# A decoder layer on one core: the first block's logits on 128 keys, and the MLP norm's factor applied after the second product

## The chip, the core and the metric

The kernel runs on one core of one Trainium2 chip. The metric is the device time of one execution in microseconds. The core has a matrix engine (TensorE, PE in the profile; PEld is its loading of weights), a vector engine (VectorE, DVE), a scalar engine for activations (ScalarE, ACT), GpSimd (POOL) and a queue that mostly issues DMAs (SyncE, SP). They run side by side and wait for each other through semaphores.

## What is computed

The layer takes 512 tokens of 1024 channels in float32. Two branches read the same RMS-normalised input: a chunkwise mLSTM with four heads, and sliding-window attention with 16 query heads, 4 key heads and learned sinks. They are merged through sigmoid gates and a projection, then come a squared-ReLU MLP, a gated per-layer embedding, and a final norm. The parts that the change touches are:

```python
def rmsnorm(x, g):
    xf = x.astype(jnp.float32)
    xf = xf * lax.rsqrt(jnp.mean(xf * xf, axis=-1, keepdims=True) + EPS)
    return xf.astype(x.dtype) * g.astype(x.dtype)

# attention: W = 128, nb = S // W = 4 blocks of queries, each against the block before and its own
logits = jnp.einsum("bnqhgd,bnkhd->bnhgqk", qb, kb).astype(jnp.float32) * (SW_HEAD_DIM ** -0.5)
diff = qi + W - ki
band_mask = (diff >= 0) & (diff < W)
valid = band_mask[None] & ((jnp.arange(nb)[:, None, None] > 0) | (ki >= W)[None])
...
# MLP
u = rmsnorm(x, norm_mlp_g[i]) @ w_up[i]              # 1024 -> 4096
x = x + jnp.square(jax.nn.relu(u)) @ w_down[i]       # 4096 -> 1024
```

The first block of queries (n = 0) has no block before it, so only the 128 keys of its own block count. In the MLP the norm's factor of a token, r = 1/sqrt(mean(x^2) + eps), is positive and the same for all channels of that token. So relu(r u)^2 = r^2 relu(u)^2, and r^2 may also multiply a token's sums after the second product.

## The kernel before

**Precision.** Nearly every large product is made from two float32r parts of each operand, a high part and the remainder. `split` makes them: ACT copies the high part (L134), DVE subtracts (L135). `pairs` lists three products per pair of tiles (high by high, high by low, low by high), and `chain` (L162) issues them all, so that one line stands for most matmuls. `load_w` loads a tile of weights and splits it; raw tiles have four buffers, and so have the parts `wh` and `wl`.

**Order.** The source's order is not the order on the engines. The tile framework plans each engine's stream from the dependencies, the free buffers and its own estimates of durations. `tc.keep_in_program_order` pins an instruction behind all that its engine has got so far, and `tc.issue_after` queues a group behind a given instruction.

**Attention.** There are 16 units: two pairs of key heads (`kp`), four blocks of 128 queries (`n`), two halves (`ab`). `swa_probs` makes the logits of one unit into a PSUM tile `ls` of 1024 columns, 256 for each of four query heads: one matmul with the high part of the keys (L608) and one with the low part (L609) per head, both over 256 keys whatever `n` is. The width `W` of what is read afterwards is 128 for n = 0 and 256 otherwise: the masked maximum on DVE (L616), the exponentials on ACT (L627), the division. `swa_out` transposes the probabilities (L645) and multiplies them by the values (L653). The units are started two ahead, with projections of other parts as filling between them.

**MLP.** Before it, `columns_of` transposes the residual `xk` (four views of the tile `XK`, 128 tokens each) and makes `x1`, scaled by the norm's gain but not by the token's factor. L852 to L860 then compute that factor: squares with a sum on ACT (L856), square root and reciprocal (`rstd_of`), a diagonal matrix from it on DVE (L858), and four products of `ones` with the diagonals (L859) that spread the factors along the columns of a PSUM tile. A copy (L860) puts them into `rB`, 128x512.

The MLP runs in four stages q, each with a first product (`up`, 1024 of the 4096 hidden channels in eight chunks of 128) and a second product (`down`). One chunk of `up` is 24 matmuls into one of two PSUM banks `psg`. L879 evicts the bank on DVE, with the relu and the factor in one instruction:

```python
V.scalar_tensor_tensor(a, ps, 0.0, rB, ALU.max, ALU.mult)
```

ACT squares the result into `F` (L883), and after every second chunk DVE makes four sums and differences in `F`, and `split` makes the operand `uf` from it. `F` has one buffer.

`down` computes a 2x2 block product with seven block products (Strassen's scheme in Winograd's form), on PSUM pairs X, Y and Z of 2 x 512 columns. When a pair holds something that belongs to a result block, `acc` adds it to the residual in one addition of 1024 columns (L916). One partial product, `p1`, is summed over all four stages in SBUF and added three times in the last stage (`acc_p1`); those additions are pinned. After the first product of the last stage, `ple_rows` loads the rows of the input `p` into memory that the MLP's scratch (`F` and `rt`) has left, and transposes them.

`cp` is the pool of small tiles that live throughout. Behind its constants it holds an unused tile `pad`.

Of the kernel before, what the change touches and what calls it, by code (L numbers as in the profile page):

```python
# [10 lines left out]
F32 = mybir.dt.float32  # L11
F32R = mybir.dt.float32r
AF = mybir.ActivationFunctionType
ALU = mybir.AluOpType
AX = mybir.AxisListType

P = 128
S = 512
D = 1024
NT = S // P  # L20
KT = D // P
EPS = 1e-6
# [14 lines left out]
def block_kernel(  # L37
# [30 lines left out]
    V, A, G, T = nc.vector, nc.scalar, nc.gpsimd, nc.tensor  # L68


    def pool(stack, name, **kw):
        return stack.enter_context(tc.tile_pool(name=name, bufs=1, reuse_waits="tile", **kw))
# [3 lines left out]
    cp = pool(ctx, "cp")  # L76
# [9 lines left out]
    def nm(s):  # L86
        n_names[0] += 1
        return f"{s}_{n_names[0]}"
# [8 lines left out]
    def ps_a():  # L97
        return pp.tile([P, 1024], F32, tag="a", bufs=2, name=nm("psa"))
# [26 lines left out]
    def small(n, w, bufs=4):  # L125
        return cp.tile([P, w], F32, tag=f"{n}{w}", bufs=bufs, name=nm(n))
# [27 lines left out]
    def pairs(a, b):  # L154

        return [(a[0], b[0]), (a[0], b[1]), (a[1], b[0])]
# [36 lines left out]
    ident = cp.tile([P, P], F32, name="ident")  # L193
    make_identity(nc, ident)
    ones = cp.tile([P, P], F32, name="ones")
    V.memset(ones, 1.0)
    eps_t = cp.tile([P, 1], F32, name="eps_t")

    cp.tile([P, 24], F32, name="pad")
    V.memset(eps_t, EPS)  # L200
    zeros4 = c1.tile([4, P], F32, name="zeros4")
    V.memset(zeros4, 0.0)
# [49 lines left out]
    def rstd_of(ss, n):  # L252

        w = ss.shape[1]
        sd = small("sd", w)
        A.activation(sd, ss, AF.Sqrt, bias=eps_t, scale=1.0 / n)
        rs = small("rs", w, 5)
        V.reciprocal(rs, sd)
        return rs
# [5 lines left out]
    for m in range(NT):  # L265
        xn = tok_scratch("xn")
        ss = small("ss", 1)
        A.activation(xn, xt[m], AF.Square, accum_out=ss)
        rs = rstd_of(ss, D)
        for c in range(2):  # L270
            o = slice(c * 512, (c + 1) * 512)
# [4 lines left out]
        for kq in range(2):  # L276
            ps = ps_t()
# [8 lines left out]
        ps = ps_g()  # L286
        for c in range(3):
            mm_tok(ps[:, :264], wv[c], hT[K3[c]], m, first=c == 0, last=c == 2)
        t = sp.tile([P, 256], F32, tag="vs", bufs=4, name=nm("vs"))
# [12 lines left out]
    kk, kl = [], []  # L302
    for i in range(2):
        ps = proj_T(w_ksw, i, ps_t)
        both = [act_r("kk"), act_r("kk")]
        low = [act_r("kl"), act_r("kl")]
        for ab in range(2):
            s, o = HALF[ab], HALF[1 - ab]
# [67 lines left out]
    for m in range(NT):  # L376
        t = tk("vm").rearrange("p (h d) -> p h d", h=NH)
# [223 lines left out]

    def swa_probs(kp, n, ab):
        k0 = max(n - 1, 0) * P
        ls = ps_a()
        for g in range(4):
            q = qs[kp * 4 + g, ab]
            o = ls[:, g * 256 : (g + 1) * 256]
            T.matmul(o, q[:, n * P : (n + 1) * P], kk[kp][ab][:, k0 : k0 + 256], start=True, stop=False)  # L608
            T.matmul(o, q[:, n * P : (n + 1) * P], kl[kp][ab][:, k0 : k0 + 256], start=False, stop=True)  # L609
        W = P if n == 0 else 2 * P  # L610
        kv = 2 * kp + ab
        sk = sink[:, kv * 4 : kv * 4 + 4]
        lm3 = tok_scratch().rearrange("p (g k) -> p g k", g=4)[:, :, :W]
        mx = small("mx", 4)
        for g in range(4):
            V.tensor_tensor_reduce(  # L616
                lm3[:, g, :], ls[:, g * 256 : g * 256 + W], band[:, 256 - W :], 0.125, sk[:, g : g + 1], ALU.add, ALU.max, mx[:, g : g + 1]
            )
        nmx = small("nmx", 4)
        V.tensor_scalar_mul(nmx, mx, -1.0)  # L620
        ds = small("ds", 4)
        V.tensor_sub(ds, sk, mx)
        es = small("es", 4)
        A.activation(es, ds, AF.Exp)
        sm = small("sm", 4)
        for g in range(4):
            A.activation(lm3[:, g, :], lm3[:, g, :], AF.Exp, bias=nmx[:, g : g + 1], accum_out=sm[:, g : g + 1])  # L627
        V.tensor_add(sm, sm, es)
        rc = small("rc", 4)
        V.reciprocal(rc, sm)  # L630
        V.tensor_tensor(lm3, lm3, rc.unsqueeze(2).broadcast_to([P, 4, W]), ALU.mult)
        probs[kp, n, ab] = lm3
# [153 lines left out]
    for i in range(8):  # L786
        ps = ps_g()
# [13 lines left out]
    XK = xp.tile([P, NT, D], F32, name="xk")  # L801
    xk = [XK[:, m, :] for m in range(NT)]
# [3 lines left out]
    def pair():  # L806

        return pp.tile([P, 2, 512], F32, tag="pair", bufs=3, name=nm("psp"))
# [13 lines left out]
    for nh in range(2):  # L822
        if nh == 0:
            a, b = pair(), pair()
            pv = [a[:, 0, :], a[:, 1, :], b[:, 0, :], b[:, 1, :]]
        else:
            a = pair()
# [5 lines left out]
        for m in range(NT):  # L833
            o = xk[m][:, nh * 512 : (nh + 1) * 512]
# [10 lines left out]
    mp = pool(st_m, "mp")  # L845
    F = lambda: mp.tile([P, 8, 256], F32, tag="F", bufs=1, name=nm("F"))

    A21, A11, A22, A12, S1, S2, S3, S4 = range(8)
    rB = mp.tile([P, 512], F32, name="rB")
    p1 = np_.tile([P, 2, 512], F32, name="p1")  # L850

    psr = pair()[:, 0, :]  # L852
    for m in range(NT):
        junk = np_.tile([P, 7 * 256], F32, tag="uf", bufs=8, name=nm("junk"))[:, :D]
        ss = small("ss", 1)
        A.activation(junk, xk[m], AF.Square, accum_out=ss)  # L856
        dg = mp.tile([P, 512], F32, tag="rt", bufs=3, name=nm("dg"))[:, :P]
        V.tensor_scalar_mul(dg, ident, rstd_of(ss, D))  # L858
        T.matmul(psr[:, m * P : (m + 1) * P], ones, dg, start=True, stop=True)  # L859
    A.copy(rB, psr)  # L860

    def load_down(q):
        raws = []
# [9 lines left out]
    def up(q, uf):  # L873
        fs = None
        for f in range(8):
            ps = ps_g()
            mm_T(ps, load_w(w_up[q * 8 + f], KT * P, KT), x1)
            a = mp.tile([P, 512], F32, tag="rt", bufs=3, name=nm("rt"))
            V.scalar_tensor_tensor(a, ps, 0.0, rB, ALU.max, ALU.mult)  # L879
            if f % 2 == 0:  # L880
                fs = F()
            o = 2 * (f % 2)
            A.activation(fs[:, o : o + 2, :].rearrange("p a b -> p (a b)"), a, AF.Square)  # L883
            if f % 2:
                hl = [np_.tile([P, 7 * 256], F32R, tag="uf", bufs=8, name=nm("uf")) for _ in range(2)]

                cut = 3 * 256 if f == 7 else 0
                if cut:
                    split([t[:, :cut] for t in hl], fs[:, 1:4, :].rearrange("p a b -> p (a b)"))
                V.tensor_add(fs[:, S1, :], fs[:, A21, :], fs[:, A22, :])  # L890
                V.tensor_sub(fs[:, S3, :], fs[:, A11, :], fs[:, A21, :])
                V.tensor_sub(fs[:, S2, :], fs[:, S1, :], fs[:, A11, :])
                V.tensor_sub(fs[:, S4, :], fs[:, A12, :], fs[:, S2, :])  # L893
                split([t[:, cut:] for t in hl], fs[:, 1 + cut // 256 :, :].rearrange("p a b -> p (a b)"))
                uf.append(hl)

    def down(q, uf):
        raws = load_down(q)
        b11, b12, b21, b22 = [[raws[4 * kh + i] for kh in range(2)] for i in range(4)]
        X, Y, Z = pair(), pair(), pair()  # L900

        def form(raw):
            return load_w(None, 1024, 2, raw)

        def prod(ps, a, w, kh, first, last):

            for t in range(2):
                o = (a - 1) * 256 + t * P
                ops = []
                for k in range(2):  # L910
                    ops += pairs([h[:, o : o + P] for h in uf[2 * kh + k]], [h[:, k, :] for h in w])
                chain(ps[:, t, :], ops, first and kh == 0, last and kh == 1, True)

        def acc(ps, toks, n):
            o = XK[:, 2 * toks : 2 * toks + 2, n * 512 : (n + 1) * 512]
            return V.tensor_add(o, ps, o)  # L916

        def acc_p1(toks, n):
            if q == 3:
                tc.keep_in_program_order(acc(p1, toks, n))  # L920

        for kh in range(2):
            V.tensor_sub(b12[kh], b22[kh], b12[kh])
        for kh in range(2):
            w = form(b11[kh])
            prod(X, A11, w, kh, True, False)
            V.tensor_add(b11[kh], b12[kh], b11[kh])
            w = form(b11[kh])
            prod(Y, S2, w, kh, True, False)
        if q == 0:  # L930
            A.copy(p1, X)
        else:
            V.tensor_add(p1, X, p1)
        acc(Y, 1, 1)
        for kh in range(2):
            w = form(b21[kh])
            prod(X, A12, w, kh, False, True)
            V.tensor_sub(b21[kh], b21[kh], b11[kh])
        acc(X, 1, 0)
        for kh in range(2):  # L940
            prod(Y, S3, form(b12[kh]), kh, False, False)
        acc(Y, 0, 1)
        acc_p1(0, 1)
        for kh in range(2):
            V.tensor_sub(b11[kh], b22[kh], b11[kh])
            prod(Z, S1, form(b11[kh]), kh, True, False)
        acc(Z, 0, 1)
        acc_p1(1, 1)
        acc_p1(0, 0)
        for kh in range(2):  # L950
            prod(Y, A22, form(b21[kh]), kh, False, True)
        acc(Y, 0, 0)
        for kh in range(2):
            prod(Z, S4, form(b22[kh]), kh, False, True)
        acc(Z, 1, 1)
# [51 lines left out]
    with tc.issue_after(evicted):  # L1007
        for m in range(NT):
            junk = tp.tile([P, D], F32, tag="junk", bufs=1, name=nm("junk"))
            ss = small("ss", 1)  # L1010
# [54 lines left out]
    a, b = pair(), pair()  # L1065
# [14 lines left out]
    for m in range(NT):  # L1080
        for o in (0, 256):
            ps = ps_g()[:, :256]
# [102 lines left out]
```

## Time and profile before

| | |
|---|---|
| median of three runs | 908.59 us (907.73, 908.59, 1108.4) |
| the profiled execution | 907.79 us, span 906.0 us |
| mean granted TensorE clock in it | 0.997 |
| TensorE busy | 890.4 us, 98% of the span |
| DVE, ACT busy | 640.6 us (71%), 452.8 us (50%) |
| traffic with HBM | 91.30 MB read, 8.40 MB written |

All durations below come from the one profiled execution, so they are to be set against its 907.79 us. Its span of 906.0 us is what the trace covers; the remaining 1.8 us lie around it. A share of busy time is an average over stages: what one stage is limited by is read in that stage. In the timelines a row has its start and its duration in microseconds, the engine, the line of the kernel, the operation, the tile written and the tiles read, and in brackets how long the engine was idle before it and what ended that.

### The profile page before, as it was taken

The numbers are of one execution on the slowest core, as the hardware profiler recorded it, in microseconds if no ns is written. First come the engines' busy times: TensorE is split into PE (matmuls) and PEld (weight loads), VectorE is DVE, ScalarE is ACT, GpSimd is POOL, SyncE is SP. The second block draws the span as 40 slices with busy tenths as digits, with TensorE's granted clock in tenths as the row PEclk, the third lists the DMA queues.
The fourth block names the chain that finished last, engine by engine and source line by source line (L and its number), as shares of the span: only waits on it lengthen the run. The fifth ranks groups of instructions, "written<-read, shape, count | busy, mean of one in ns | idle before, by whom it ended". The sixth has DMA issues, their size and how long they took to land.

```text
span 906.0 us, 11754 instructions
## 1 busy us (share of the span) xinstructions
PE 890.4 (98%) x4490; PEld 739.4 (82%) x4490; DVE 640.6 (71%) x1020; ACT 452.8 (50%) x757; POOL 25.0 (3%) x44
## 2 busy tenths in 40 slices
PE   7999999999999999999999999999999999999996
PEld 5888889998877677777888888888888888888886
DVE  6684687874787977466654678857966895799556
ACT  6573444454677567564322545334434533454753
POOL 0011000000000000000210000000000000000000
PEclk9999999999999999999999999999999999999998
DMA  6644124435211122234452520531162044201402
GB/s 235 241 156 151 59 81 167 162 117 173 71 49 69 47 96 92 76 110 140 163 186 93 207 95 1 198 127 47 54 225 94 0 159 146 69 24 64 145 1 93
DMA packets 30346, 101.51 MB, mean 112 GB/s; under 512 B 4301, under 2 KB 4813, under 8 KB 30290
## 3 DMA queue, kind: packets, MB, share of 16 engines
q1 hardware_dynamic: 28002, 93.15, 29.9%
q0 software_dynamic: 2144, 7.35, 2.3%
q8 instruction: 35, 0.57, 0.2%
q10 hardware_dynamic: 144, 0.26, 0.1%
q14 instruction: 21, 0.17, 0.1%
HBM read 91.30 MB, written 8.40 MB: 110 GB/s over the span
## 4 chain that ended last, share of the span: by engine, by line
PE 93%; ACT 2%; DVE 2%; DMA 1%; issue 0%; SPq 0%; ACTq 0%; DVEq 0%
PE psg L162 51%; PE psp L162 23%; PE psa L162 10%; PE pst L724 2%; PE pst L653 1%; PE pst L162 1%; PE psa L645 1%; PE pst L714 1%; PE psa L608 1%; PE psa L609 1%; DMA xt<-in_x 1%; DMA gfin<-in_g_fin 1%; PE psp L817 1%; ACT jk L736 1%; ACT pT L647 0%
## 5 line engine op out<-in xcount | busy, mean ns | idle before, releaser
L134 ACT CAST wh<-wr 128x1024 fp32r<-128x1024 f32 (+1 forms) x137 | 142.9, 1046 | 207.7 <-PE psg L162 75.4
L135 DVE TENSOR_TENSOR wl<-wr,wh 128x1024 fp32r<-128x1024 f32 (+1 forms) x137 | 173.4, 1270 | 102.4 <-ACT wh L134 95.4
L162 PE MATMUL psg<-x,wh 128*128 128x512 f32 x512 | 158.4, 390 | 0.0
L162 PE MATMUL psp<-wh,uf 128*128 128x512 f32 x448 | 139.2, 390 | 0.0
L162 PEld LDWEIGHTS psg<-x,wh 128*128 128x128 f32 x512 | 96.1, 188 | 19.8
L162 PE MATMUL psg<-h,wh 128*128 128x512 f32 x320 | 101.3, 395 | 0.0
L162 PE MATMUL psg<-x,wl 128*128 128x512 f32 x256 | 99.7, 390 | 0.0
L162 PEld LDWEIGHTS psp<-wh,uf 128*128 128x128 f32 x448 | 84.1, 188 | 17.4
L162 PE MATMUL psp<-wl,uf 128*128 128x512 f32 x224 | 87.3, 390 | 0.0
L134 ACT CAST wh<-wd 128x1024 fp32r<-128x1024 f32 x44 | 46.3, 1054 | 58.0 <-PE psp L162 26.1
L162 PEld LDWEIGHTS psg<-h,wh 128*128 128x128 f32 x320 | 58.8, 188 | 15.9 <-issue 4.9
L162 PE MATMUL psg<-h,wl 128*128 128x512 f32 x160 | 62.9, 393 | 0.0
L135 DVE TENSOR_TENSOR wl<-wd,wh 128x1024 fp32r<-128x1024 f32 x44 | 53.5, 1219 | 4.4 <-ACT wh L134 4.1
L162 PEld LDWEIGHTS psg<-x,wl 128*128 128x128 f32 x256 | 48.1, 188 | 9.8
L162 PE MATMUL psa<-h,wh 128*128 128x256 f32 (+1 forms) x256 | 55.2, 312 | 0.0
L162 PEld LDWEIGHTS psp<-wl,uf 128*128 128x128 f32 x224 | 42.1, 188 | 8.6
L135 DVE TENSOR_TENSOR uf<-F,uf 128x1792 fp32r<-128x1792 f32 (+2 forms) x20 | 33.0, 1650 | 21.8 <-ACT uf L134 21.8
L162 PEld LDWEIGHTS psa<-h,wh 128*128 128x128 f32 x256 | 41.9, 191 | 3.5 <-ACT p L533 0.7
L162 PE MATMUL psg<-yb,wh 128*128 128x512 f32 x128 | 42.8, 409 | 0.0
L134 ACT CAST uf<-F 128x1792 fp32r<-128x1792 f32 (+2 forms) x20 | 27.9, 1395 | 26.4 <-DVE F L893 26.2
L162 PE MATMUL psg<-ya,wh 128*128 128x512 f32 x128 | 40.6, 394 | 0.0
L879 DVE SCALAR_TENSOR_TENSOR rt<-psg,rB 128x512 f32<-128x512 f32 x32 | 22.0, 688 | 25.6 <-PE psg L162 25.6
(273 smaller groups left out, 1673.3 us busy)
## 6 DMA issues: line engine op xcount, KB each, us to landing
wr<-in_w_up SPq DMA_DIRECT2D x32, 512.0 KB, 3.2
wd<-in_w_down SPq DMA_DIRECT2D x24, 512.0 KB, 3.8
wr<-in_w_o SPq DMA_DIRECT2D x8, 512.0 KB, 4.5
gd<-gr POOLq DMA_DIRECT2D x8, 512.0 KB, 2.9
wr<-in_w_qsw SPq DMA_DIRECT2D x8, 512.0 KB, 4.3
wr<-in_w_qkml SPq DMA_DIRECT2D x8, 512.0 KB, 3.3
wr<-in_w_b SPq DMA_DIRECT2D x8, 512.0 KB, 3.2
gl<-gd SPq DMA_DIRECT2D x8, 512.0 KB, 3.4
```

The lines of the kernel that those rows point to most:

```text
L134: A.copy(dst[0], src)
L135: V.tensor_sub(dst[1], src, r32(dst[0]))
L162: last_mm[0] = T.matmul(ps, l, r, start=first and i == 0, stop=last and i == len(ops) - 1, skip_group_check=parts)
L608: T.matmul(o, q[:, n * P : (n + 1) * P], kk[kp][ab][:, k0 : k0 + 256], start=True, stop=False)
L609: T.matmul(o, q[:, n * P : (n + 1) * P], kl[kp][ab][:, k0 : k0 + 256], start=False, stop=True)
L645: T.transpose(pt[:, c : c + P], lm3[ab][:, g, j * P : (j + 1) * P], ident)
L653: T.matmul(o[HALF[ab], :], vs[n + 1 - nk + j][:, c : c + 64], pTs[j][:, ab * 512 : (ab + 1) * 512], start=j == 0, stop=j == nk - 1,)
L714: T.matmul(psc[:, n0:], qk[4 + h][:, n0 : n0 + P], qk[h][:, n0:], start=True, stop=True)
L724: T.matmul(pn[:, : DV + 1], wT[s][:, t * P : (t + 1) * P], vm[s][:, h, :], start=s == 0, stop=s == t)
L736: A.activation(jk[:, :DV], h_of(h, t), AF.Square, scale=rd[:, t : t + 1], accum_out=hss[:, h, t : t + 1])
L817: T.transpose(ps[:, m * P : (m + 1) * P], xk[m][:, k * P : (k + 1) * P], ident)
L879: V.scalar_tensor_tensor(a, ps, 0.0, rB, ALU.max, ALU.mult)
```

## The change

Three things are edited. The logits' matmuls of the first block cover 128 keys instead of 256. The factor r is no longer spread over `rB`: its square is kept as one column per 128 tokens in a new tile `r2` (computed as the reciprocal of mean plus eps, without a square root), `up` evicts with a plain relu on ACT instead of DVE, and `acc` multiplies each token's sums by `r2` while adding them, in two instructions of 512 columns, one per 128 tokens, instead of one of 1024. `pad` shrinks by eight columns, about what `r2` takes.

```diff
@@ -196,7 +196,7 @@
-    cp.tile([P, 24], F32, name="pad")
+    cp.tile([P, 16], F32, name="pad")
@@ -601,13 +601,13 @@
     def swa_probs(kp, n, ab):
         k0 = max(n - 1, 0) * P
+        W = P if n == 0 else 2 * P
         ls = ps_a()
         for g in range(4):
             q = qs[kp * 4 + g, ab]
-            o = ls[:, g * 256 : (g + 1) * 256]
-            T.matmul(o, q[:, n * P : (n + 1) * P], kk[kp][ab][:, k0 : k0 + 256], start=True, stop=False)
-            T.matmul(o, q[:, n * P : (n + 1) * P], kl[kp][ab][:, k0 : k0 + 256], start=False, stop=True)
-        W = P if n == 0 else 2 * P
+            o = ls[:, g * 256 : g * 256 + W]
+            T.matmul(o, q[:, n * P : (n + 1) * P], kk[kp][ab][:, k0 : k0 + W], start=True, stop=False)
+            T.matmul(o, q[:, n * P : (n + 1) * P], kl[kp][ab][:, k0 : k0 + W], start=False, stop=True)
@@ -846,18 +846,16 @@
-    rB = mp.tile([P, 512], F32, name="rB")
     p1 = np_.tile([P, 2, 512], F32, name="p1")
-    psr = pair()[:, 0, :]
+    r2 = cp.tile([P, NT], F32, name="r2")
     for m in range(NT):
         junk = np_.tile([P, 7 * 256], F32, tag="uf", bufs=8, name=nm("junk"))[:, :D]
         ss = small("ss", 1)
         A.activation(junk, xk[m], AF.Square, accum_out=ss)
-        dg = mp.tile([P, 512], F32, tag="rt", bufs=3, name=nm("dg"))[:, :P]
-        V.tensor_scalar_mul(dg, ident, rstd_of(ss, D))
-        T.matmul(psr[:, m * P : (m + 1) * P], ones, dg, start=True, stop=True)
-    A.copy(rB, psr)
+        V.tensor_scalar(ss, ss, 1.0 / D, EPS, ALU.mult, ALU.add)
+        V.reciprocal(r2[:, m : m + 1], ss)
@@ -876,7 +874,7 @@
             a = mp.tile([P, 512], F32, tag="rt", bufs=3, name=nm("rt"))
-            V.scalar_tensor_tensor(a, ps, 0.0, rB, ALU.max, ALU.mult)
+            A.activation(a, ps, AF.Relu)
@@ -911,13 +909,14 @@
-        def acc(ps, toks, n):
-            o = XK[:, 2 * toks : 2 * toks + 2, n * 512 : (n + 1) * 512]
-            return V.tensor_add(o, ps, o)
+        def acc(ps, toks, n, pin=lambda i: None):
+            for t in range(2):
+                o = xk[2 * toks + t][:, n * 512 : (n + 1) * 512]
+                pin(V.scalar_tensor_tensor(o, ps[:, t, :], r2[:, 2 * toks + t : 2 * toks + t + 1], o, ALU.mult, ALU.add))
         def acc_p1(toks, n):
             if q == 3:
-                tc.keep_in_program_order(acc(p1, toks, n))
+                acc(p1, toks, n, tc.keep_in_program_order)
```

## The prediction

> **What bounds the kernel now.** I read the head of the profile first, then the chain that ended last in order of time, then the busy time by stage, and last the timelines around each edit.
>
> ```profile
> span 906.0 us, 11754 instructions
> PE 890.4 (98%) x4490; PEld 739.4 (82%) x4490; DVE 640.6 (71%) x1020; ACT 452.8 (50%) x757; POOL 25.0 (3%) x44
> ...
> 516.78 37.88 PE psg L162 x167
> 554.67 38.08 PE psp L162 x168
> 592.75 43.52 PE psg L162 x192
> ...
> 838.82 5.82 DMA gfin<-in_g_fin
> ```
>
> TensorE is busy for 98% of the span, and through the whole MLP the chain consists of its matmuls alone: chunk after chunk, stage after stage, without a gap. The row with 192 matmuls in 43.52 us gives the price of one 512-column matmul in a stream: 226.7 ns. One chunk of the first product (24 matmuls) takes 5.44 us, one step of the second product (12) takes 2.72 us. In the MLP, then, an edit saves time only by taking work from TensorE, and costs time only if it makes TensorE wait. How full the others are there (columns PE, PEld, DVE, ACT, POOL; one first product, then the last second product):
>
> ```profile
> 592.75:636.26 43.51, 43.51 (x193) 36.04 (x193) 29.60 (x35) 17.74 (x19) 0.00 (x0) 1.00 0.21 73
> 799.47:838.82 39.35, 39.33 (x178) 32.23 (x178) 36.62 (x41) 18.55 (x25) 0.00 (x0) 1.00 0.18 56
> ```
>
> ACT has room in the first product (17.74 of 43.51 us). DVE has 13.9 us of room there, but only 2.7 us in the last second product. The granted clock is 1.00.
>
> **Part 1, the row factors (L849 to L860).** Eight TensorE records go (four plain float32 products of `ones` with a diagonal, two records each). They lie in the stream of the first chunks:
>
> ```profile
> 513.96 0.62 PE L162 MATMUL psg<-x,wh 128*128 128x512 f32 x2
> 514.42 0.61 PE L859 MATMUL psp<-dg,ones 128*128 128x128 f32 x4
> 514.78 0.47 PE L162 MATMUL psg<-x,wl 128*128 128x512 f32 x1
> 515.09 0.62 PE L162 MATMUL psg<-x,wh 128*128 128x512 f32 x2
> 515.55 0.40 PE L162 MATMUL psg<-x,wl 128*128 128x512 f32 x1
> 515.83 0.49 PE L859 MATMUL psp<-dg,ones 128*128 128x128 f32 x2
> 516.08 0.48 PE L162 MATMUL psg<-x,wh 128*128 128x512 f32 x1
> 516.39 0.39 PE L859 MATMUL psp<-dg,ones 128*128 128x128 f32 x2
> 516.54 0.48 PE L162 MATMUL psg<-x,wh 128*128 128x512 f32 x1
> 516.86 0.40 PE L162 MATMUL psg<-x,wl 128*128 128x512 f32 x1
> 517.09 0.62 PE L162 MATMUL psg<-x,wh 128*128 128x512 f32 x2
> ```
>
> From 513.96 to 517.09 are 3.13 us, in which nine matmuls of 226.7 ns start (2.04 us). The rest, 1.09 us, is what the eight records and the joints around them cost: **-1.1 us**, all on the path. The same edit takes four square roots and the copy to `rB` from ACT and four multiplications by the diagonal from DVE; the new affine step and reciprocal on 128x1 are as small as the ones that go. They lie beside the stream and count as nothing either way.
>
> **Part 2, the logits of the first block.** For n = 0 there are four units (two head pairs times two halves) of eight matmuls: 32 matmuls go from 256 to 128 columns. Their spacing now, and the nearest row with 128 columns and a fresh weight load for each:
>
> ```profile
> 230.75 0.28 PE L608 MATMUL psa<-kk,qs 128*128 128x256 f32 x1
> 230.87 0.28 PE L609 MATMUL psa<-kl,qs 128*128 128x256 f32 x1
> 230.99 0.28 PE L608 MATMUL psa<-kk,qs 128*128 128x256 f32 x1
> ...
> 245.08 0.87 PE psa L645 x8
> ```
>
> One of 256 columns starts every 120 ns. The eight transposes of L645 take 0.87 us, 109 ns each. No row shows this float32r kind with fewer than 256 columns, so I bound it. If only the columns counted, 60 ns: 32 x 60 = -1.9 us. If the kind lost its single pass at this width and went like plain float32, the row of the diagonal at 515.83 is the nearest: two records, one product of 128 columns, 0.25 us until the next start, 32 x 0.13 = +4.2 us. I take 109 ns, the row with the same 128 columns and a load per matmul: 32 x 11 ns = **-0.35 us**. VectorE and ACT already work on 128 keys there (`W` is 128 for n = 0), so they change nothing.
>
> The Trainium skill ("TensorE: Matmul & The Clock Gate", Back-to-back issue gap) puts a sustained load and matmul pair of 128 columns at about 81 ns. By that figure, an estimate, this part would bring 32 x 39 ns = 1.25 us. The transposes here show 109 ns, so the trace does not reach the page's figure, at least for four-byte operands.
>
> **Part 3, the relu goes from DVE to ACT.** 32 evictions of 688 ns leave DVE. On ACT the nearest row is a copy of the same shape from PSUM, 588 ns:
>
> ```profile
> L879 DVE SCALAR_TENSOR_TENSOR rt<-psg,rB 128x512 f32<-128x512 f32 x32 | 22.0, 688 | 25.6 <-PE psg L162 25.6
> L883 ACT ACTIVATE F<-rt 128x512 f32<-128x512 f32 x32 | 20.1, 628 | 20.7 <-DVE rt L879 20.7
> L995 ACT COPY pe<-psg 128x512 f32<-128x512 f32 x8 | 4.7, 588 | 3.7 <-PE psg L162 3.6
> ```
>
> ACT then carries 17.74 + 8 x 0.59 = 22.5 of 43.5 us in a first product. What decides is when a bank of `psg` is free again. The order inside one odd chunk, whose matmuls end near 603.5 (ACT rows, then DVE):
>
> ```profile
> 603.48 1.05 ACT L134 CAST wh<-wr 128x1024 fp32r<-128x1024 f32 x1 [3.90 <-issue]
> 604.44 0.62 ACT L883 ACTIVATE F<-rt 128x512 f32<-128x512 f32 x1
> 607.14 1.70 ACT L134 CAST uf<-F 128x1792 fp32r<-128x1792 f32 x1 [2.07 <-DVE F L893]
> ...
> 603.66 0.69 DVE L879 SCALAR_TENSOR_TENSOR rt<-psg,rB 128x512 f32<-128x512 f32 x1 [3.02 <-PE psg L162]
> ...
> 605.71 0.42 DVE L890 TENSOR_TENSOR F<-F 128x256 f32<-128x256 f32 x1
> ```
>
> In the new order I put the relu behind the cast that starts at 603.48: 604.5 to 605.1, the square to 605.7. The sums on DVE start at 605.71 even now, so the chain to the next operand moves by about nothing. The bank is free 1.6 us after its last matmul; it is needed 5.44 us after, when the neighbour bank's chunk has ended. Behind the waiting relu stand the casts of later weights; they wait for the end of the same chunk anyway, and four buffers lie ahead of TensorE. After a chunk with the 1.70 us cast the relu comes some 2 us later, still inside. So **0**, covered by 5.44 us of matmuls per chunk. Without that cover it would be 32 x 0.59 = 19 us.
>
> The Trainium skill ("ScalarE: Activation LUTs", Rules for kernel authors) advises VectorE for relu, up to about 3 times faster in bf16. In float32 from PSUM the rows here stand the other way round, 588 against 688 ns. By the page a relu would cost ACT up to 2.1 us (an estimate), 34 of 43.5 us per first product: dearer, but still covered.
>
> **Part 4, the sums into `xk` (L916).** Each 1024-wide addition (24 from PSUM, three from `p1`) becomes two 512-wide multiply-adds. Two adjacent 512-wide rows on the same engine show the price, beside the present one:
>
> ```profile
> 505.38 1.29 DVE L835 TENSOR_TENSOR xk<-psp,xk 128x512 f32<-128x512 f32 x2 [0.41 <-PE psp L162]
> ...
> 838.82 1.23 DVE L916 TENSOR_TENSOR xk<-psp,xk 128x1024 f32<-128x1024 f32 x1 [0.41 <-PE psp L162]
> ```
>
> That is +0.06 us each; with 0.69 us apiece and no overlap it would be +0.15. For nine of them in the last second product this is 0.5 to 1.4 us of the 2.7 us that DVE has there; the weights are split one to two steps of 2.72 us ahead. The very last sum, at 838.82, has TensorE working on the first four columns and the DMA of `gfin` beside it. Here I take 0.
>
> **Part 5, the end of the last first product.** One thing hangs on the moved relu there. The rows of `p` reuse the memory of `F`, so their load starts when the last split of `F` is done, and TensorE already waits for it:
>
> ```profile
> 804.71 1.23 DVE L135 TENSOR_TENSOR uf<-F,uf 128x1024 fp32r<-128x1024 f32 x1
> ...
> 805.96 1.78 SPq L963 DMA_DIRECT2D ptok<-in_p  x4
> ...
> PEld psg L966 <- DMA ptok<-in_p: 0.3, 1, 0.3
> ```
>
> The relu (0.59) ahead of the square pushes this split by some 0.4 us, where no DVE work hides it; the eviction that DVE no longer does gives some back. Between 0 and +0.6 us, I take **+0.3**.
>
> **Sum.** -1.1 - 0.35 + 0.3 = -1.15 us. The profiled execution took 907.79 us (span 906.0), so 906.6 on its own scale. The two runs near it are 907.73 and 908.59, the second being the median beside a far longer third; their middle, 908.16, gives **907.0 us**. The rest of the kernel is taken to keep its order.
>
> **The rivals.**
> *The logits are dearer at 128 columns.* Part 2 at its upper bound: 907.0 + 0.35 + 4.16 = 911.5, slower than before. It decides as soon as one of these takes over 155 ns (32 x 35 ns outweigh the 1.1 us). For it: the plain float32 rows show that a matmul here can need several passes, and every float32r row has at least 256 columns. Against it: the rows of 256 and of 512 columns shown here cost one pass (120 and 226.7 ns).
>
> *ACT lets go of the bank too late.* The planner could queue a relu behind the cast that waits for the end of the following chunk. The bank is then free at 5.44 + 1.05 + 0.59 = 7.08 us and TensorE stands for 1.64 us. In the 16 odd chunks that is 26 us, 933; it passes 2% (18 us) from 11 such chunks. For it: today's order does put a cast ahead of the square. Against it: that cast starts at the same moment as the eviction, and ACT has 21 us free per first product.
>
> *Relu and square alternate tables.* Table loads here take 1283 ns. If the relu needed another table than the square, two loads per chunk would bring ACT to 17.74 + 8 x (0.59 + 2.57) = 43.0 of 43.5 us, and with its waits for DVE it would bound the stage: some 2 us per odd chunk, 32 us, 939.
>
> ```profile
> L256 ACT ACT_TABLE_LOAD x2 | 2.6, 1283 | 0.0
> ```
>
> The Trainium skill ("ScalarE: Activation LUTs", Table sets) says that cheap functions such as relu lie in every set. By that this rival falls; no row of this profile holds a relu on ACT, so I leave it 1 in 100.
>
> *The planner reorders attention.* Shorter matmuls early on can shift which cast or exponential comes first between 228 and 340 us, where ACT and DVE, too, end pieces of the chain:
>
> ```profile
> 306.98 1.48 ACT lm L627 x6
> 309.25 0.95 ACT wh L134
> ```
>
> A few such pieces more or fewer are 4 us either way: 903 or 911.
>
> **How the numbers follow.** The forecast 0.50, dearer logits 0.22, reordered attention 0.16, late banks 0.11, tables 0.01. The forecast's own bounds (part 2 alone to -1.9, part 5 from 0 to 0.6, the spread of the runs) are 904.5 to 908.5. Taking in the second and the fourth case, the range is 903.5 to 914; what is left out is late banks, tables and the ends. More than 2% faster would need 18 us that TensorE does not have to give: 0.01. Late banks, tables and a bad order make up slower by more than 2%, 0.12; the rest, 0.87, is within 2%, about what a measurement of this kernel can tell from no change.
>
> **What would show it.** Right: no record of the diagonal product, 192 matmuls in 43.52 us in each first product, relu rows near 590 ns on ACT starting 0 to 3 us after their chunk, pairs of 512-wide sums at 1.3 us, first-block logits spaced about 109 ns. Wrong: logits spaced 155 ns or more, TensorE waiting for ACT at `psg`, table loads between 517 and 800 us, or a wait for `ptok` of over 1 us.

## The result and the profile after

The change made the kernel slightly slower: a median of 910.51 us over 15 runs, against 907.29 us for the kernel before beside it. The ratio of the fast runs (one run of the kernel before, of 1108.4 us, is a slow one) is 1.0031, with a 95% interval of 1.0023 to 1.0039, that is +2.8 us; the two medians lie 3.2 us apart. The forecast was 907.0, about 1 us below the 908.16 that it took for the kernel before. The time lies inside the stated range and within 2%, but the sign is wrong, and the interval leaves no doubt of it. The profiled execution took 910.05 us, with a granted clock of 0.998 against 0.997 before.

The head of the profile after, and the chain of waits in order of time (start, duration, engine, tile, line, number of pieces):

```profile
span 908.3 us, 11743 instructions
PE 889.2 (98%) x4482; PEld 738.3 (81%) x4482; DVE 625.9 (69%) x1015; ACT 469.6 (52%) x784; POOL 25.0 (3%) x44
...
207.92 21.57 PE psg L162 x95
...
464.57 21.76 PE psp L162 x96
...
555.63 38.08 PE psp L162 x168
593.71 43.52 PE psg L162 x192
...
840.54 6.56 DMA gfin<-in_g_fin
...
856.41 21.76 PE psp L162 x96
```

TensorE has less to do, 889.2 us instead of 890.4, and the span is 2.3 us longer: the new time is time in which it stands. The same pieces of the chain exist in the kernel before, so they serve as marks. Three of its rows were not shown yet:

```profile
208.17 21.79 PE psg L162 x96
...
462.51 21.76 PE psp L162 x96
...
853.91 21.76 PE psp L162 x96
```

The marks are: A, the last stream of projections before attention begins to mix with it (207.92); B, the output projection after attention (464.57); C, the first second product of the MLP (555.63); G, the end of the last second product, where the load of `gfin` is issued (840.54); L, the second product of the part with `p` (856.41); and the end of the span. Subtracting neighbours gives the time by stretch:

| stretch | before | after | difference |
|---|---|---|---|
| start to A | 208.17 | 207.92 | -0.25 |
| A to B: attention | 254.34 | 256.65 | +2.31 |
| B to C: output, norm, first product | 92.16 | 91.06 | -1.10 |
| C to G: the rest of the MLP | 284.15 | 284.91 | +0.76 |
| G to L: the tail with `gfin` | 15.09 | 15.87 | +0.78 |
| L to the end | 52.09 | 51.89 | -0.20 |

Executions of the same code at the start put A anywhere from 206.98 to 209.32 us in the runs below. So the comparisons that follow use stretches and medians, and not spans.

**What came as forecast.** The factor's eight records are gone and B to C is 1.10 us shorter. The relu on ACT, as a group (count, then busy us and mean ns, then idle time ahead of it) and inside one odd chunk (ACT's timeline):

```profile
L877 ACT ACTIVATE rt<-psg 128x512 f32<-128x512 f32 x32 | 18.9, 589 | 0.5 <-PE psg L162 0.5
...
604.40 1.06 ACT L134 CAST wh<-wr 128x1024 fp32r<-128x1024 f32 x1 [3.23 <-PE psg L162]
605.35 0.59 ACT L877 ACTIVATE rt<-psg 128x512 f32<-128x512 f32 x1
605.97 0.64 ACT L881 ACTIVATE F<-rt 128x512 f32<-128x512 f32 x1
```

It takes 589 ns, starts 0.95 us after the start of the cast, and the square follows it at once. The first products still take 43.52 us for 192 matmuls (the row at 593.71), so no bank comes late. The sums take longer than I had put; the views list the durations (minimum, median, maximum) of the 512-wide sums, one pair of them on DVE's timeline, and the busy time of a first product and of the last second product (PE, PEld, DVE, ACT, POOL):

```profile
L915 DVE SCALAR_TENSOR_TENSOR xk<-psp,r,xk x48: 741/745/752, 567.8 to 841.2; 128x512 f32<-128x512 f32 x48
...
840.55 1.41 DVE L915 SCALAR_TENSOR_TENSOR xk<-psp,r,xk 128x512 f32<-128x512 f32 x2
...
593.71:637.23 43.52, 43.52 (x193) 36.04 (x193) 25.31 (x29) 21.62 (x26) 0.00 (x0) 1.00 0.22 73
800.26:840.54 40.28, 40.01 (x181) 32.70 (x180) 37.38 (x48) 19.15 (x26) 0.00 (x0) 1.00 0.15 42
```

ACT stands at 21.62 of 43.52 us. In the last second product DVE is busy for 37.38 of 40.28 us, a little more than before (36.62 of 39.35).

**What came unforeseen, in attention.** TensorE's timeline of the first block, after:

```profile
230.61 0.27 PE L609 MATMUL psa<-kk,qs 128*128 128x128 f32 x1
230.72 0.28 PE L610 MATMUL psa<-kl,qs 128*128 128x128 f32 x1
230.83 0.45 PE L162 MATMUL psg<-h,wh 128*128 128x512 f32 x1
232.64 0.33 PE L609 MATMUL psa<-kk,qs 128*128 128x128 f32 x1 [1.35 <-DVE qs L573]
```

The logits start 110 ns apart, close to the 109 ns that I took. But TensorE then stands for 1.35 us and waits for the copy of the fourth head's queries. Before, at the same place:

```profile
232.89 0.39 PE L608 MATMUL psa<-kk,qs 128*128 128x256 f32 x1
```

There is no wait there. The DVE rows say that the copy itself is not late; first after, then before:

```profile
231.90 0.68 DVE L573 TENSOR_TENSOR qs<-psg,qs 64x512 fp32r<-64x512 f32 x1
```

```profile
232.15 0.69 DVE L573 TENSOR_TENSOR qs<-psg,qs 64x512 fp32r<-64x512 f32 x1
```

It comes at 231.90 where it came at 232.15. What changed is TensorE's order. The two programs' instructions side by side (not from the trace; numbers of the tiles at the end of the names; some rows of equal kind left out):

```
 L162 MATMUL psg_2267<-h_135,wh_2270 128x512
+L609 MATMUL psa_2207<-kk_396,qs_2201 128x128
+L610 MATMUL psa_2207<-kl_398,qs_2201 128x128
 L162 MATMUL psg_2267<-h_136,wh_2270 128x512
 L162 MATMUL psg_2267<-h_135,wl_2271 128x512
 L162 MATMUL psg_2267<-h_135,wh_2270 128x512
 L162 MATMUL psg_2267<-h_136,wh_2270 128x512
...
-L608 MATMUL psa_2207<-kk_396,qs_2201 128x256
-L609 MATMUL psa_2207<-kl_398,qs_2201 128x256
```

The planner that writes TensorE's order put the logits of the fourth head behind one filling matmul (one that belongs to a projection); before, there were seven. The filling work that used to cover the copy now stands behind the wait.

### The profile page after: what moved, and what is told of

The parts are those of the page before. It is cut to its first block, busy times and chain, and to the rows that moved or that the text cites. A ratio compares the mean times of both kernels' runs of the same rounds, so it can differ in the third digit from the quotient of the medians.

```text
span 908.3 us, 11743 instructions
## 1 busy us (share of the span) xinstructions
PE 889.2 (98%) x4482; PEld 738.3 (81%) x4482; DVE 625.9 (69%) x1015; ACT 469.6 (52%) x784; POOL 25.0 (3%) x44
## 4 chain that ended last, share of the span: by engine, by line
PE 90%; ACT 4%; DVE 3%; DMA 2%; issue 0%; SPq 0%; ACTq 0%; DVEq 0%
PE psg L162 49%; PE psp L162 22%; PE psa L162 10%; PE pst L724 2%; PE pst L653 1%; PE pst L162 1%; PE pst L714 1%; ACT lm L627 1%; PE psa L645 1%; DMA gfin<-in_g_fin 1%; DMA xt<-in_x 1%; ACT pT L647 1%; ACT wh L134 1%; PE psa L609 1%; PE psp L817 1%; ACT jk L736 1%
## 5 line engine op out<-in xcount | busy, mean ns | idle before, releaser
L162 PE MATMUL psa<-h,wl 128*128 128x256 f32 (+1 forms) x128 | 39.6, 309 | 0.0
```

The costliest lines, as they stand in the source:

```text
L162: last_mm[0] = T.matmul(ps, l, r, start=first and i == 0, stop=last and i == len(ops) - 1, skip_group_check=parts)
```

## The experiments

The theory after the result: the time is lost by the order in attention and not by the width; the MLP's half brings 1.1 us and loses about as much at its end. The rivals: the narrower logits themselves are dearer; the relu on ACT is what costs. All ratios are to the kernel before on the same chip. The two halves alone came first, with two kernels that hold the order fixed.

**e1, the attention half alone.** The edit of lines 601 to 613 of the diff, and nothing else.

```diff
+        W = P if n == 0 else 2 * P
...
-            o = ls[:, g * 256 : (g + 1) * 256]
+            o = ls[:, g * 256 : g * 256 + W]
...
```

> Only the attention edit (logits of the first block on 128 keys), the MLP as before. Theory O (the loss in attention comes from the new order in which the engines' instructions stand): the stage up to the first product of the MLP ends some 2 us later, as in the trace of after (464.6 against 462.5 us at the output projection); time about +2 us against before. Theory C (the matmuls themselves are dearer or the change costs nothing here): with 110 ns spacing seen in the trace, -0.35 us.

Measured: 910.93 us against 907.17, ratio 1.0043 (1.0029 to 1.0057). The chain:

```profile
208.11 21.57 PE psg L162 x95
...
464.75 21.76 PE psp L162 x96
```

A to B takes 256.64 us, as in the whole change (256.65; before 254.34). This half is where the loss comes from.

**e2, 128 columns in the order of before.** The same edit; in attention, each instruction of TensorE, ACT and DVE is tied behind the one that came ahead of it in the kernel before (the code is shortened here and below: the lists of instructions are left out, and each engine has its own).

```diff
+    for earlier, later in zip(order_of_before, order_of_before[1:]):
+        tc.add_manual_dep(by[later], earlier, NoSync, reason="replayed order")
```

> The attention edit with 128 columns, but all instructions of TensorE, ACT and DVE in attention are held in the order in which before has them. Theory O: the loss is gone, about -0.4 us against before (32 matmuls of 110 instead of 120 ns). Theory C, or a loss that lies in shorter matmuls reaching a wait earlier: as the attention edit alone, +2 us, or 0.

**e3, 256 columns in the new order.** The reverse: the logits stay 256 wide everywhere, and attention follows the order that the planner chose for e1.

```diff
+    for earlier, later in zip(order_of_e1, order_of_e1[1:]):
+        tc.add_manual_dep(by[later], earlier, NoSync, reason="replayed order")
```

> Before with its 256 columns everywhere, but held in the order that the planner chose for the attention edit on TensorE, ACT and DVE. Theory O: it is slow although nothing in it is changed but the order: about +2.3 us against before. Theory C: no difference to before, 0 +- 0.5 us.

Measured: e2 907.08 us, ratio 1.0000 (0.9991 to 1.0008); e3 909.80 us, ratio 1.0029 (1.0019 to 1.0039). The chains of e2 and of e3, and e3's largest new wait of TensorE between 225 and 425 us (total, times, longest):

```profile
209.32 21.79 PE psg L162 x96
...
463.05 21.76 PE psp L162 x96
```

```profile
207.51 21.57 PE psg L162 x95
...
463.96 21.76 PE psp L162 x96
...
PE psa L608 <- DVE qs L573: 1.3, 1, 1.3
```

A to B is 253.73 us in e2, 0.6 less than before, and 256.45 in e3, 2.1 more. This settles where the loss comes from. The order alone, with before's matmuls, brings the wait for the queries and the loss; the narrower matmuls alone bring a little in this stretch (forecast: -0.35), and e2's median can't be told from before. The rival of dearer logits falls.

**e4, the MLP half alone.** Everything of the diff below line 846.

```diff
-            V.scalar_tensor_tensor(a, ps, 0.0, rB, ALU.max, ALU.mult)
+            A.activation(a, ps, AF.Relu)
...
```

> Only the MLP edit. From the two traces: -1.1 us for the eight records of the diagonal product, +0.8 us in the last second product (rows of p later), +0.6 us behind the load of gfin: about +0.2 us against before. If the last two are not the edit's doing but follow from the shift in attention, -1.1 us.

Measured: 907.79 us, ratio 1.0005 (0.9996 to 1.0013): no difference. The chain from C on:

```profile
553.35 38.08 PE psp L162 x168
...
832.69 0.45 PE psg L162 x2
...
838.39 5.70 DMA gfin<-in_g_fin
...
853.40 21.76 PE psp L162 x96
```

C to G takes 285.04 us, 0.9 more than before, which gives back most of the 1.1 us won ahead of C. G to L is 15.01 us here, less than in the whole change; the load of `gfin` landed after 5.70 us and not after 6.56.

**e5, the first wait undone.** e1 again, in its own order but for the stretch around the wait of 1.35 us (16 matmuls, among them the fourth head's logits of two units, and two pieces each on ACT and DVE), which has before's order. The edit in words:

```diff
-order_of_e1
+order_of_e1, with the first stretch that differs taken from order_of_before
```

> The attention edit alone, in the planner's new order, except its first stretch of differences: the logits of the fourth head of units 0 and 1 stand again behind the six filling matmuls where before has them. If the 1.35 us for which TensorE waits there for the copy of the queries (DVE) is what costs, some 1.3 us of the loss of the attention edit are gone and some 0.7 us stay. If the loss is spread over the later stretches, or an early wait is caught up later, the time stays where the attention edit alone has it (+2 to +4 us against before).

Measured: 908.60 us against 907.40, ratio 1.0014 (1.0006 to 1.0023). The chain:

```profile
207.96 21.79 PE psg L162 x96
...
463.00 21.76 PE psp L162 x96
```

A to B is 255.04 us. Of the 2.3 us, 1.6 belong to that one place; 0.7 (1.3 against e2, which has the same width) are spread over later stretches, where ACT's and DVE's pieces enter the chain more often than before. A second, separate loss shows here: in e1, e3 and e5, L to the end takes 52.8 us instead of 52.1, with the last store of `z` landing 3.6 us after its issue instead of 2.7. It is some 0.7 us of what these three lose against before, and the whole change doesn't have it. What makes the store slower in those three I have not tested.

**e6, the whole change with attention in before's order.**

```diff
+    for earlier, later in zip(order_of_before, order_of_before[1:]):
+        tc.add_manual_dep(by[later], earlier, NoSync, reason="replayed order")
```

> The whole change, with attention held in the order of before. Theory O: the loss in attention goes, what stays is the logits' -0.35, the diagonal product's -1.1 and the tail's cost: between -1.5 and +0.3 us against before, and 2 to 3 us below the changed kernel (910.5).

**e7, the same with the relu on DVE.**

```diff
-            A.activation(a, ps, AF.Relu)
+            V.tensor_scalar_max(a, ps, 0.0)
```

> As the one before it, but the relu stays on DVE (a maximum with 0, 688 ns or a little less). If the relu on ACT is what makes the rows of p late in the last stage, their load is issued again 6.5 us after the end of the first product (6.6 to 6.8 with the relu on ACT) and the wait behind it is 0.4 us shorter. If it is only the spread of that load's duration, nothing moves: the same time as the kernel before it within 0.5 us.

Measured: e6 907.59 us against 907.40, ratio 1.0005 (0.9995 to 1.0014); e7 907.01, ratio 1.0001 (0.9989 to 1.0012). Without the new order in attention the change makes no difference that can be told: the loss of the median goes with that order. Nor do the medians tell e6 and e7 apart. In the chains (e6, then e7):

```profile
552.12 38.08 PE psp L162 x168
...
753.40 43.31 PE psg L162 x191
...
837.00 6.54 DMA gfin<-in_g_fin
...
852.84 21.76 PE psp L162 x96
```

```profile
552.84 38.08 PE psp L162 x168
...
754.12 43.52 PE psg L162 x192
...
837.23 6.67 DMA gfin<-in_g_fin
...
853.21 21.76 PE psp L162 x96
```

C to G is 284.88 us in e6 and 284.39 in e7, 0.5 us more with the relu on ACT, in one execution each. The last first product begins 201.28 us behind C in both (753.40 and 754.12), so all of it falls behind that point, where the rows of `p` are waited for. G to L is 15.84 and 15.98 us. So the loss from G to L is not the relu's. In all of these G to L is the landing of `gfin` and 9.3 us behind it (15.84 - 6.54, 15.98 - 6.67, 15.01 - 5.70 in e4, 15.09 - 5.82 before): the two scalings of `gfin` stand on DVE ahead of splits of `x2`, and these wait with them.

**e8, early rows of p and late scalings.** On top of e6, two of the four tiles of `p` are loaded ahead of the last first product into memory of their own, and the scalings of `gfin` go behind the last split of `x2`.

```diff
+    ptok = [np_.tile([P, PLE], F32, tag="ptok", bufs=2, name=nm("ptok")) for _ in range(2)]
...
+        if q == 3:
+            for m in range(2):
+                nc.sync.dma_start(out=ptok[m], in_=p[m * P : (m + 1) * P, :])
...
+    with tc.issue_after(last_split[0].ins):
+        V.tensor_scalar_mul(glast, gfin, D**0.5 / 8192)
+        V.tensor_scalar_mul(gfin, gfin, -(D**0.5) / 8192)
```

> The whole change with attention held in the order of before, and two edits at its end: the first two tiles of p are loaded before the last first product into memory of their own, and the two scalings of gfin on DVE stand behind the last split of x2, so that no split waits for the load of gfin. The waits for ptok and for the splits (0.4 and 0.6 us in the MLP edit alone) go: 0.8 to 1.5 us below the whole change in the old order, and 1.5 to 3 us below before. If those waits vary by themselves from run to run, no difference of the kernels beyond 0.5 us.

Measured: 906.74 us, ratio 0.9995 (0.9987 to 1.0004): not told from before, where 1.5 to 3 us less had been expected. G to L fell to 14.84 us, but C to G was 285.00 (e6: 284.88). TensorE's only wait of this view between 755 and 860 us:

```profile
PE psp L163 <- DVE wl L135: 0.8, 1, 0.8
```

The early rows of `p` moved the planner's order once more and brought a wait for a split of the weights, which stands on DVE behind four of the 512-wide sums in a row. One edit hid what the other gave, so I ran the scalings alone.

**e9, late scalings alone, on e6.**

```diff
-    V.tensor_scalar_mul(glast, gfin, D**0.5 / 8192)
-    V.tensor_scalar_mul(gfin, gfin, -(D**0.5) / 8192)
...
     evicted = ple(1, load_w(w_pp[1], 2 * 512, 2))
+    with tc.issue_after(last_split[0].ins):
+        V.tensor_scalar_mul(glast, gfin, D**0.5 / 8192)
+        V.tensor_scalar_mul(gfin, gfin, -(D**0.5) / 8192)
```

> The whole change, attention held in the order of before, and only one edit at the end: the two scalings of gfin stand on DVE behind the last split of x2. If splits that stand behind the wait for gfin are what eats the gain of the MLP edit, the stretch from the second product of stage 0 to the last product of the gate (322.0 to 322.5 us with the MLP edit, 320.7 to 321.2 without) falls by some 0.9 us to 321.5, the waits of TensorE for x2 (1.3 us) go, and the median lies 0.5 to 1.2 us below the whole change in the old order. If the planner's other order of the products with p is what costs, not the wait, the stretch stays at 322.4.

**e10, the same with the relu on DVE.** e9 and the line of e7.

```diff
-            A.activation(a, ps, AF.Relu)
+            V.tensor_scalar_max(a, ps, 0.0)
```

> As the kernel before it, with the relu on DVE. The row load of p is then issued 6.5 us after the end of the first product and the wait behind it shrinks: another 0.3 to 0.5 us, the stretch at 321.0 to 321.2, about 1.5 us below before in all. If the relu's engine does not matter at the end: as the kernel before it.

**e11, late scalings in the kernel before.** The edit of e9, and nothing of the change.

> Before with the same one edit to the scalings of gfin. In before TensorE waits 0.2 us there, so -0.2 to -0.3 us: the late scalings by themselves are worth little without the MLP edit. If they were worth 0.9 us here too, the wait would not be the MLP edit's.

Measured, against 906.95 us: e9 905.02, ratio 0.9982 (0.9973 to 0.9991); e10 904.72, ratio 0.9977 (0.9968 to 0.9985); e11 907.42, ratio 1.0002 (0.9993 to 1.0010). The chain of e9, where the piece behind the last second product is now transposes and not a load, and then DVE's rows (a split of `x2`, the scalings behind it):

```profile
552.30 38.08 PE psp L163 x168
...
836.93 0.87 PE psp L818 x8
...
851.26 21.76 PE psp L163 x96
```

```profile
845.00 2.07 DVE L138 SCALAR_TENSOR_TENSOR x<-psp,gple,x 128x512 fp32r<-128x512 f32 x3 [2.82 <-ACT x L137]
...
848.90 0.69 DVE L1004 TENSOR_SCALAR glast<-gfin 128x1024 f32<-128x1024 f32 x1
```

G to L is 14.33 us, 1.5 below e6. e10 has 14.34 us, and 284.34 instead of 284.63 us from C to G. In e11 the same edit leaves G to L at 15.00 us (837.62 to 852.62; before 15.09) and the median where it was. So the scalings were almost free in the kernel before, and in the changed one they cost 1.5 us where the load takes 6.5 us. How much depends on that load: in e4, where it took 5.70 us, G to L is 15.01 us, only 0.7 above e9. e10, with the late scalings, attention in before's order and the relu back on DVE, is 0.23% below the kernel before; e9's interval overlaps its own.

## Why the prediction was wrong, by its own steps

**The base.** The forecast started from 908.16 us, the middle of two runs; the median of 15 is 907.29. By its own terms it said -1.15 us, and against that median its 907.0 is only 0.3 us less.

**Part 1 (-1.1): right.** B to C is 1.10 us shorter after, and in e4 (91.06 us), e6 and e9 alike.

**Part 2 (-0.35): right for the matmuls themselves.** They start 110 ns apart, and the kernels with 128 columns in before's order (e2, e6 to e10) are 0.2 to 0.7 us shorter than before from A to B. The Trainium skill's figure of 81 ns ("TensorE: Matmul & The Clock Gate", Back-to-back issue gap) is not reached at this width and kind: 110 ns.

**Part 3 (0): right.** 589 ns against the 588 taken from the copy; the square starts 1.6 us after the start of the cast, the first products keep their 43.52 us, and ACT has 21.62 us per first product (forecast 22.5).

**Part 4 (0): the price was mis-sized, and the place where I named only the cover was the place where it broke.** A pair of sums costs 1.41 us and not 1.29, so it adds 0.18 us and not the 0.06 to 0.15 that I put. That mattered little here: TensorE has no wait for a split of weights between 555 and 836 us. But the last sum was set at nothing because TensorE works on the first four columns while the load of `gfin` runs beside it. TensorE's and DVE's rows there, first after, then before:

```profile
848.53 0.66 PE L817 MATMUL psp<-ident,xk 128*128 128x128 f32 x4 [0.76 <-DVE x L138]
849.79 0.66 PE L817 MATMUL psp<-ident,xk 128*128 128x128 f32 x4 [0.60 <-DVE x L138]
...
847.12 0.69 DVE L987 TENSOR_SCALAR glast<-gfin 128x1024 f32<-128x1024 f32 x1 [2.68 <-DMA gfin<-in_g_fin]
847.73 0.74 DVE L138 SCALAR_TENSOR_TENSOR x<-psp,gple,x 128x512 fp32r<-128x512 f32 x1
```

```profile
847.33 0.66 PE L817 MATMUL psp<-ident,xk 128*128 128x128 f32 x4 [0.20 <-DVE x L138]
...
844.66 0.69 DVE L988 TENSOR_SCALAR glast<-gfin 128x1024 f32<-128x1024 f32 x1 [2.16 <-DMA gfin<-in_g_fin]
```

After, DVE stands for 2.68 us until `gfin` has landed, the split behind it is late, and TensorE stands twice, 1.36 us in all; before, it stood for 0.20. Two parts make up the difference. The planner moved two products with `p` (the row of 0.45 us at 832.69 in e4) from behind G to ahead of it, so less work is left to cover the load. That is 0.45 us more from C to G and would have been 0.45 less from G to L; G to L rose by 0.78 instead. The remainder is the load itself, which took 0.74 us longer than before. e9 and e11 show that the wait for `gfin` is the cause: with the MLP's half it costs 0.7 us (e4, load of 5.70 us) to 1.6 (e7, 6.67), and without it 0.1 at most, since in before, e1, e2, e3 and e5 G to L is 15.01 to 15.09 us with loads of 4.5 to 5.8 us, against 15.00 in e11. The longer load is not shown to be the change's: over the seven executions with the MLP's half it took 4.8 to 6.7 us, over the six without it 4.5 to 5.8. What makes it long stays open.

**Part 5 (+0.3): the size is near, but it is not shown to be the relu's.** In the four executions with the relu on ACT and this load as it was (after, e4, e6, e9), the load of `p` is issued 50.1 us after the start of the last first product; in the eight with it on DVE it is 50.0. So the relu pushes it by 0.1 us and not by 0.4. C to G is longer with the relu on ACT, by 0.5 us in e6 against e7 and by 0.3 in e9 against e10. But e1 and e5, both with the old eviction, differ by 0.5 us there too (284.45 and 283.91), and e1 has the same wait of TensorE for these rows (total, times, longest) as after, where it is 0.27 us:

```profile
PE psg L966 <- DMA ptok<-in_p: 0.4, 1, 0.4
```

These are single executions, and the medians don't separate them.

**The step that failed is the last sentence of the sum: "The rest of the kernel is taken to keep its order."** The forecast terms came out near what was put, at -1.1, some -0.5 and +0.1 to +0.5. To them came the new order of attention, from A to B +2.1 us at 256 columns (e3 against before) and +2.9 at 128 (e1 against e2), and some +1.2 us around G (0.45 and 0.74), where the planner's order changed too and the load came later. The rival of a reordered attention, given 0.16 and 911 us, is what happened, in the stretch it named. Its price was near, but only in part by its reason: it counted pieces of ACT and DVE in the chain, which fits the 1.3 us of the later stretches, and the larger part (1.6 us) is one place where TensorE waits, made by logits put six matmuls too early. That the price came out near is partly luck. The other rivals fell: logits at 155 ns or more (110), late banks (43.52 us unchanged) and alternating tables. No table load lies between 517 and 800 us after, as the Trainium skill says of relu ("ScalarE: Activation LUTs", Table sets).

## What to carry to other kernels

Where a planner writes the order from its own costs, a small edit is two edits: the work, and a new order. Here, with TensorE 98% busy, the second was larger than the first and turned the forecast -1.15 us into +2.8. Hold the order fixed in one experiment (new work in the old order) and the work fixed in another (old work in the new order) before a loss is put down to an instruction. And where a cover is named in a prediction, count how much of it stays when its neighbours move: the scalings of `gfin` cost 0.1 us before and 1.5 after, by lost cover and by a longer load, and the change did not touch them.

## What the runs showed of the hardware

- Matmuls of this float32r kind with 128 columns and a load each start 110 ns apart, against 120 ns at 256 columns and 226.7 ns at 512. Halving 256 columns brings almost nothing.
- A multiply-add of 512 columns from PSUM with a factor per partition takes 745 ns on DVE and 1.41 us for two, where a plain addition of 1024 takes 1.23 us.
- A relu of 128x512 from PSUM takes 589 ns on ACT, the same as a copy (588).
- The load of `gfin` at the end of the last second product landed after 4.5 to 6.7 us over the thirteen kernels' profiled executions, and the start of the kernel up to mark A varied by 2.3 us between executions of the same instructions. A difference of one stretch of one execution of this size at a load is no evidence of a cause.
